# One addend instead of two in the norm of group B, and priority for its chain and for the out projection's additions

## The chip, the cores and the metric

The kernel runs on one core of one Trainium2 chip. The metric is the device time of one execution in microseconds (us); lower is better. In the text, TensorE (PE) multiplies matrices, VectorE (DVE) does elementwise work, ScalarE (ACT) does activations and casts, GpSimd (POOL) helps with elementwise work, and SyncE (SP) issues most DMA transfers. Each engine works through its own instructions in a fixed order and waits on semaphores for the others.

## The reference

One encoder layer on an input of 1 x 1024 tokens x 1024 channels, in float32. What matters here is the middle of it: two attention groups of 512 channels each, an RMS norm for each group, one out projection, and the residual sum.

```python
hn = rmsnorm(h, norm_mix[l])
proj = jnp.einsum('bsd,de->bse', hn, w_in[l])
...
o_a = window_gqa_sink(qa, ka, va, sink[l])
o_b = neighbourhood_attention(qb, kb, vb, rpb[l])
mix = jnp.concatenate([rmsnorm(o_a, norm_a[l]), rmsnorm(o_b, norm_b[l])], axis=-1)
h = h + jnp.einsum('bse,ed->bsd', mix, w_out[l])
hn = rmsnorm(h, norm_ffn[l])
h = h + conv_gated_mlp(hn, w_gate[l], w_up[l], conv_w[l], conv_b[l], w_down[l])
```

where `rmsnorm(x, g)` is `x * rsqrt(mean(x * x) + 1e-6) * g` over the channels.

## The kernel before, in words

Channels lie on the 128 partitions and the 1024 tokens along the free axis, in two halves of 512 (`tsl(h)`). Each float32 matmul is done as three fast ones: an operand is split into a high part (a cast on ScalarE) and a low part (a subtraction on VectorE), and a **block** is the three products high x high, high x low, low x high, each 128x512 (L113 to L115). A product of four blocks makes one half of one output tile out of 512 input channels, in one PSUM bank.

The order on TensorE is written by hand. The other four engines' orders are made by a planner at build time, which takes the instructions by priority (normally program order) as soon as its own model says that they are ready; a piece inside `tc.high_priority(offset=500)` is taken as if it stood 500 places earlier. Whatever order it makes is then fixed, and an engine waits at each instruction until that one may run.

**Attention with filler.** While the attention units of groups A and B run, a generator (`rest`, `fill(n)`) puts blocks of other matmul work between them. First these are the input projections, and at the end `OutA`, the half of the out projection that belongs to group A: for each of eight output tiles d it takes two products (halves h = 0, 1) of `mg[0:4]`, each into a bank of the tag `pj`, of which there are two. The addition at L490 reads the bank, adds the input tile `xr` (loaded by a DMA at L486), writes `h1[d]` and so frees the bank for the product after the next.

**Norm of group B.** `mix[4]` to `mix[7]` hold the four tiles of group B. Their squares are summed in `square_b` (L700 to L707) into `sums["b"]` for tiles 4 to 6; the squares of the last tile go into `last` (L744 to L746). `inverse_narrow` (L145) sums over the channels on TensorE: for each of four groups of 128 tokens it multiplies every addend with a column of ones, giving one column each (L150), then takes the square root on ScalarE (L153) and the reciprocal on VectorE (L154). `widen` (L157) spreads the result over 128 partitions by four more matmuls (L161). The norm itself is at L765 to L767: on VectorE a scaling of `mix[4 + i]` that reads the wide result, on ScalarE the cast to the high part `mg[4 + i]`, on VectorE the subtraction for the low part, for four tiles in each half.

The hand-written order around it, on TensorE, is: the last attention matmul, five blocks of `OutA` (`fill(5)`, L756), the sums of both halves (L757), four blocks (`fill(4)`), `widen` of half 0, three blocks (`fill(3)`), `widen` of half 1, and then all blocks of `OutA` that are left.

**Group B's out projection.** After that (loop of L857) come sixteen products of `mg[4:8]` with the other half of `w_out`, for half 0 and then for half 1, in six banks; L816 adds each to `h1[d]`, L819 and L821 square and sum for the next norm. The weights for d = 0 and 1 are loaded early (`load_wo`, L748), those from d = 2 on into memory that the attention stage gives back. In the same loop, and after it, the first weights of the gated MLP are made: `pure` loads and splits `w_gate`, and `head_weights` forms sums of `w_gate` and `w_up` blocks on VectorE (L843, L835). The MLP follows, and it is matmul after matmul to the end.

Of the kernel before, what the change touches and what calls it, by code (L numbers as in the profile page):

```python
# [15 lines left out]
AF = mybir.ActivationFunctionType  # L16
ALU = mybir.AluOpType
# [34 lines left out]
def hybrid_layer(tc, xT, w_in, w_out, w_gate, w_up, w_down, small, sink, rpb, consts, rope, out):  # L52
    nc = tc.nc
    with ExitStack() as ctx:
# [13 lines left out]
        def big(name, tag, dt=F32):  # L68
            return lpool.tile([128, S], dt, name=name, tag=tag, bufs=slots[tag])

        def tmp(name, dt=F32, n=S):
            return tpool.tile([128, n], dt, name=name, tag="t", padded_shape=[128, S + 2])

        def bank(name, tag):
            return psum.tile([128, HALF], F32, name=name, tag=tag)

        f32 = lambda ap: ap.bitcast(F32)
        tsl = lambda h: slice(h * HALF, (h + 1) * HALF)
# [38 lines left out]
        def product(ps, ws, xs, h):  # L117

            for i, (w, x) in enumerate(zip(ws, xs, strict=True)):
                block(ps, w, x, h, i == 0, i == len(ws) - 1)  # L120
                yield
# [23 lines left out]
        def inverse_narrow(sqs, dim, tag):  # L145

            ps = bank("ss", tag)
            for c in range(4):
                for i, sq in enumerate(sqs):
                    nc.tensor.matmul(ps[:, c:c + 1], sq[:, c * 128:(c + 1) * 128], ones[:, 0:1], start=c == 0 and i == 0,  # L150
                                     stop=i == len(sqs) - 1, skip_group_check=True)
            v = cpool.tile([128, 4], F32, name="v4", tag="v4", bufs=4)
            nc.scalar.activation(v, ps[:, 0:4], AF.Sqrt, bias=eps, scale=float(D) / dim)  # L153
            nc.vector.reciprocal(v, v)  # L154
            return v
# [86 lines left out]
        mix = [None] * 8  # L242
# [200 lines left out]
        mg, h1, norm = [None] * 8, [None] * KT, {}  # L443

        class Project:
# [6 lines left out]
            def run(self):  # L452
                self.t = tmp("t")
                if self.m < 17:
                    for h in range(2):
                        ps = bank("pj", "pj")
                        yield from product(ps, self.w, xg, h)
                        evacuate(self.t, ps, h, self.grid)
                else:

                    ps = [bank("pj", "pj") for _ in range(2)]
                    for k in range(KT):
                        for h in range(2):
                            block(ps[h], self.w[k], xg[k], h, k == 0, k == KT - 1)
                            yield
                        if k % 2:
                            mg[k // 2] = split(mix[k // 2], "mg", "xg")
                    for h in range(2):
                        evacuate(self.t, ps[h], h, self.grid)
# [5 lines left out]
        class OutA:  # L475
# [6 lines left out]
            def run(self):  # L482
                d = self.d
                h1[d] = big("h1", "mix" if d < 4 else "op")
                xt = tmp("xr")
                nc.sync.dma_start(xt, xT[d])  # L486
                for h in range(2):
                    ps = bank("pj", "pj")
                    yield from product(ps, self.w, mg[0:4], h)
                    nc.vector.tensor_tensor(h1[d][:, tsl(h)], ps, xt[:, tsl(h)], op=ALU.add)  # L490

            def post(self):
                pass
# [1 line left out]
        def fill(jobs):  # L495
            jobs[0].load()
            before = None
            for i, job in enumerate(jobs):
                if i + 1 < len(jobs):
                    jobs[i + 1].load()  # L500
                for n, _ in enumerate(job.run()):
                    yield
                    if n == LAG and before is not None:
                        before.post()
                        before = None
                before = job
            before.post()
# [190 lines left out]
        sums = {}  # L698
# [43 lines left out]


        last = tmp("sq")  # L744
        for h in range(2):
            nc.scalar.activation(last[:, tsl(h)], mix[7][:, tsl(h)], AF.Square)  # L746

        def load_wo(d, pools):  # L748
            raw = pools.tile([128, 4, 128], F32, name="raw", tag="raw", bufs=2 if pools is wpool else 3, padded_shape=[128, 4 if pools is wpool else 8, 128])
# [4 lines left out]
            return [(t[:, 0, j, :], t[:, 1, j, :]) for j in range(4)]  # L754

        fill(5)  # L756
        vb2 = [inverse_narrow([sums["b"][:, tsl(h)], last[:, tsl(h)]], 512, "pt") for h in range(2)]  # L757
        fill(4)
        mg[4:8] = [(big("mgh", "xg", F32R), big("mgl", "xg", F32R)) for _ in range(4)]
        for h in range(2):  # L760
# [96 lines left out]
        for h in range(2):  # L857
            for d in range(KT):
                if h == 0 and d + 2 < KT:
                    wo.append(load_wo(d + 2, fpool))  # L860
                ps = bank("pj", ("o", "s", "pj")[(h * KT + d) % 3])
# [365 lines left out]
        for i, (p, j, c) in enumerate(order):  # L1227
# [6 lines left out]
            ps = banks[p, j]  # L1234
# [118 lines left out]
```

## Time and profile before

| | |
|---|---|
| median of 3 runs | 1128.92 us (1128.06 to 1130.89) |
| the profiled execution, its own time | 1127.34 us |
| its span in the profile | 1125.6 us |
| TensorE busy | 96% of the span |
| VectorE busy | 76% |
| ScalarE busy | 49% |

Three views of the profile are used. The windows view gives, for a stretch of the span, how long each engine was busy in it, with the number of its instructions, the granted TensorE clock (1.00 is full), and the DMA load. The timeline lists instructions by start; where one sat behind idle time of its engine, brackets give that idle time and what ended it. The issues view lists DMA transfers with their size and their time to landing. All times in the views are microseconds from the start of the span.

### The profile page before, as it was taken

The page shows a single profiled execution, that of the slowest core. Times are in us where ns is not written, and L with a number is a line of the kernel's source. Part 1 is how long each engine was busy: PE and PEld are TensorE (multiplying, and loading weights), DVE is VectorE, ACT ScalarE, POOL GpSimd, SP SyncE. Part 2 cuts the span into 40 slices and gives each one's busy share as a digit, 9 for nine tenths or more (in the row PEclk, how much of TensorE's full clock was granted, in tenths as well). Part 3 has the DMA queues.
Part 4 walks back from the last instruction along what each step waited for, and adds up shares of the span by engine and source line. Part 5 has one row for each costly group of instructions (what it writes and reads, how often), then busy time and mean ns, then how long its engine had stood idle before and what let it go on. Part 6 is the DMA issues. An engine that isn't in the chain of part 4 may idle for free.

```text
span 1125.6 us, 14912 instructions
## 1 busy us (share of the span) xinstructions
PE 1086.2 (96%) x5124; PEld 903.0 (80%) x5124; DVE 852.4 (76%) x1549; ACT 548.3 (49%) x1033; POOL 105.7 (9%) x186
## 2 busy tenths in 40 slices
PE   8969999999999999999999999999999999999995
PEld 6858888888878877888788888888888878888884
DVE  6557888766689666989988778877877868797843
ACT  7235767655667433445434334334343645543531
POOL 0212332233223100000000000000000000000001
PEclk8989999999999999999999999999999999999997
DMA  7253220333215316412443223222322799875823
GB/s 266 65 122 80 53 57 29 84 92 87 75 31 148 103 47 211 163 47 78 166 160 122 105 92 123 102 103 94 122 103 94 244 302 294 268 221 174 272 83 144
DMA packets 67708, 147.03 MB, mean 131 GB/s; under 512 B 8112, under 2 KB 16816, under 8 KB 67632
## 3 DMA queue, kind: packets, MB, share of 16 engines
q1 hardware_dynamic: 57552, 121.04, 34.6%
q10 hardware_dynamic: 10080, 25.04, 5.9%
q8 instruction: 40, 0.66, 0.2%
q14 instruction: 36, 0.29, 0.1%
HBM read 103.58 MB, written 28.57 MB: 117 GB/s over the span
## 4 chain that ended last, share of the span: by engine, by line
PE 86%; DVE 7%; DMA 3%; ACT 2%; issue 2%; SPq 0%; POOLq 0%; ACTq 0%; DVEq 0%
PE pj L113 7%; PE pj L114 7%; PE pj L115 7%; PE dn L797 6%; PE dn L799 6%; PE dn L798 6%; PE z L799 5%; PE z L797 5%; PE z L798 5%; PE x L797 3%; PE x L799 3%; PE x L798 3%; PE s L273 3%; PE y L799 3%; PE y L797 3%; PE y L798 3%
## 5 line engine op out<-in xcount | busy, mean ns | idle before, releaser
L797 PE MATMUL dn<-xd,whi 128*128 128x512 f32 x308 | 120.2, 390 | 1.1 <-ACT c L1218 1.1
L786 ACT ACTIVATE whi<-ws 128x512 fp32r<-128x512 f32 (+1 forms) x100 | 60.1, 622 | 123.9 <-DVE ws L903 76.3
L799 PE MATMUL dn<-xd,wlo 128*128 128x512 f32 x308 | 119.8, 389 | 0.0
L798 PE MATMUL dn<-xd,whi 128*128 128x512 f32 x308 | 119.8, 389 | 0.0
L799 PE MATMUL z<-hg,wlo 128*128 128x512 f32 x264 | 103.1, 390 | 0.7 <-DVE wlo L787 0.7
L113 PE MATMUL pj<-xgh,whi 128*128 128x512 f32 x248 | 103.4, 417 | 0.0
L797 PE MATMUL z<-hg,whi 128*128 128x512 f32 x264 | 102.9, 390 | 0.0
L798 PE MATMUL z<-hg,whi 128*128 128x512 f32 x264 | 102.7, 389 | 0.0
L299 ACT ACTIVATE p<-p,nm 128x385 f32<-128x385 f32 (+3 forms) x128 | 75.1, 586 | 56.3 <-DVE nm L295 52.3
L115 PE MATMUL pj<-xgh,wlo 128*128 128x512 f32 x248 | 97.7, 394 | 0.0
L114 PE MATMUL pj<-xgl,whi 128*128 128x512 f32 x248 | 97.5, 393 | 0.0
L303 POOL TENSOR_SCALAR p<-p,sm 128x384 f32<-128x384 f32 (+1 forms) x128 | 73.5, 588 | 237.3 <-DVE sm L301 218.2
L787 DVE TENSOR_TENSOR wlo<-raw,whi 128x512 fp32r<-128x512 f32 (+1 forms) x102 | 66.3, 669 | 22.7 <-ACT whi L786 22.5
L787 DVE TENSOR_TENSOR wlo<-ws,whi 128x512 fp32r<-128x512 f32 (+1 forms) x100 | 66.7, 681 | 19.5 <-ACT whi L786 19.5
L309 DVE TENSOR_TENSOR pl<-pt,ph 128x384 fp32r<-128x384 f32 (+2 forms) x108 | 63.1, 588 | 23.2 <-ACT ph L308 22.1
L786 ACT ACTIVATE whi<-raw 128x512 fp32r<-128x512 f32 (+1 forms) x102 | 60.4, 611 | 41.4 <-DMA raw<-in_w_down_dram 18.4
L1108 ACT ACTIVATE xd<-xd 128x512 fp32r<-128x512 f32 x77 | 47.3, 627 | 58.0 <-DMA xd<-x 56.5
L308 ACT ACTIVATE ph<-pt 128x384 fp32r<-128x384 f32 (+2 forms) x108 | 55.3, 514 | 38.2 <-PE pt L408 30.8
L1209 POOL TENSOR_TENSOR y<-y,wide 128x512 f32<-128x512 f32 x4 | 5.1, 1283 | 727.0 <-ACT y L1208 727.0
L799 PE MATMUL y<-hg,wlo 128*128 128x512 f32 x176 | 68.7, 390 | 0.5 <-DVE wlo L787 0.5
L797 PE MATMUL x<-hg,whi 128*128 128x512 f32 x176 | 68.7, 390 | 0.0
L799 PE MATMUL x<-hg,wlo 128*128 128x512 f32 x176 | 68.5, 389 | 0.0
(199 smaller groups left out, 2657.8 us busy)
## 6 DMA issues: line engine op xcount, KB each, us to landing
xd<-x SPq DMA_DIRECT2D x77, 256.0 KB, 5.1
raw<-in_w_down_dram SPq DMA_DIRECT2D x72, 256.0 KB, 3.4
raw<-in_w_gate_dram SPq DMA_DIRECT2D x22, 512.0 KB, 3.5
raw<-in_w_up_dram SPq DMA_DIRECT2D x22, 512.0 KB, 4.0
x<-c ACTq DMA_DIRECT2D x22, 512.0 KB
raw<-in_w_in_dram SPq DMA_DIRECT2D x32, 256.0 KB, 3.2
raw<-in_w_down_dram SPq DMA_DIRECT2D x36, 192.0 KB, 3.8
x<-t ACTq DMA_DIRECT2D x11, 512.0 KB, 2.6
```

The source lines that it names most:

```text
L113: nc.tensor.matmul(ps, w[0], x[0][:, tsl(h)], start=first, stop=False)
L114: nc.tensor.matmul(ps, w[0], x[1][:, tsl(h)], start=False, stop=False)
L115: nc.tensor.matmul(ps, w[1], x[0][:, tsl(h)], start=False, stop=last)
L299: nc.scalar.activation(p[:, j, 0:e], p[:, j, 0:e], AF.Exp, bias=nm, scale=-1.0, accum_out=sm[:, j:j + 1])
L303: nc.gpsimd.tensor_scalar(p[:, i, 0:m], p[:, i, 0:m], sm[:, i:i + 1], 1.0, op0=ALU.mult, op1=ALU.mult)
L308: nc.scalar.activation(ph[:, 0:n], ps[:, 0:n], AF.Copy)
L309: nc.vector.tensor_tensor(pl[:, 0:n], ps[:, 0:n], f32(ph[:, 0:n]), op=ALU.subtract)
L786: nc.scalar.activation(hi, src, AF.Copy)
L787: nc.vector.tensor_tensor(lo, src, f32(hi[:, :, :]), op=ALU.subtract)
L797: nc.tensor.matmul(ps, w[0], x[0], start=first and i == 0, stop=False, skip_group_check=True)
L798: nc.tensor.matmul(ps, w[0], x[1], start=False, stop=False, skip_group_check=True)
L799: nc.tensor.matmul(ps, w[1], x[0], start=False, stop=last and i == len(ws) - 1, skip_group_check=True)
```

## The change

Three edits. The squares of the last tile are added to `sums["b"]` on VectorE, half by half, so that `inverse_narrow` has one addend for each half instead of two. The squares, these additions, and the chain of sums, square roots and reciprocals stand in `tc.high_priority(offset=500)`. So does each of `OutA`'s additions.

```diff
@@ OutA.run
                     ps = bank("pj", "pj")
                     yield from product(ps, self.w, mg[0:4], h)
-                    nc.vector.tensor_tensor(h1[d][:, tsl(h)], ps, xt[:, tsl(h)], op=ALU.add)
+                    with tc.high_priority(offset=500):
+                        nc.vector.tensor_tensor(h1[d][:, tsl(h)], ps, xt[:, tsl(h)], op=ALU.add)
@@ norm of group B
         last = tmp("sq")
-        for h in range(2):
-            nc.scalar.activation(last[:, tsl(h)], mix[7][:, tsl(h)], AF.Square)
+        with tc.high_priority(offset=500):
+            for h in range(2):
+                nc.scalar.activation(last[:, tsl(h)], mix[7][:, tsl(h)], AF.Square)
+                nc.vector.tensor_tensor(last[:, tsl(h)], last[:, tsl(h)], sums["b"][:, tsl(h)], op=ALU.add)
...
         fill(5)
-        vb2 = [inverse_narrow([sums["b"][:, tsl(h)], last[:, tsl(h)]], 512, "pt") for h in range(2)]
+        with tc.high_priority(offset=500):
+            vb2 = [inverse_narrow([last[:, tsl(h)]], 512, "pt") for h in range(2)]
         fill(4)
```

## The prediction

> **What bounds the kernel now.** I read the page's engine totals first, then the chain that ended last by engine, then the waits, and last the windows and the timeline of the stretch that the change touches.
>
> ```profile
> PE 1086.2 (96%) x5124; PEld 903.0 (80%) x5124; DVE 852.4 (76%) x1549; ACT 548.3 (49%) x1033; POOL 105.7 (9%) x186
> PE 86%; DVE 7%; DMA 3%; ACT 2%; issue 2%; SPq 0%; POOLq 0%; ACTq 0%; DVEq 0%
> ```
>
> TensorE is the bound: busy for 96% of the span, and 86% of the chain. Time can come only from where TensorE works slowly or waits. The next table is the windows view of TensorE alone, cut at the starts of its groups: sums of group B's norm (L150), four `OutA` blocks, first widening, three blocks, second widening, two blocks of output tile 6, half 1 (with a wait), four blocks of tile 7, half 0, a hole, four blocks of tile 7, half 1, and the first product with `mg[4:8]`.
>
> ```profile
> 403.35:407.00 3.65, 3.65 (x33) 0.95 0.20 75
> 407.00:411.26 4.26, 4.26 (x13) 0.64 0.34 123
> 411.26:412.07 0.81, 0.81 (x9) 1.00 0.00 0
> 412.07:414.23 2.16, 2.16 (x12) 1.00 0.00 0
> 414.23:415.04 0.81, 0.81 (x9) 1.00 0.00 0
> 415.04:416.94 1.90, 1.64 (x10) 1.00 0.00 0
> 416.94:420.00 3.06, 3.05 (x12) 1.00 0.00 0
> 420.00:423.18 3.18, 0.00 (x1) 1.00 0.00 0
> 423.18:427.63 4.45, 4.45 (x12) 0.62 0.00 0
> 427.63:430.35 2.72, 2.72 (x13) 1.00 0.51 165
> ```
>
> The columns are the length of the stretch, TensorE's busy time with its instructions, the granted clock, and the DMA load. Twelve matmuls take 2.72 us at full clock (0.68 a block), but 4.26 and 4.45 us at granted clocks of 0.64 and 0.62. Both slow stretches follow one without full-width matmuls: 3.65 us of one-column sums, and a hole of 3.18 us. The hole, as the timeline tells, ends with an addition:
>
> ```profile
> 423.18 0.50 PE L113 MATMUL pj<-mgh,whi 128*128 128x512 f32 x1 [3.18 <-DVE h L490]
> ```
>
> ```profile
> 401.51 0.69 DVE L490 TENSOR_TENSOR h<-pj,xr 128x512 f32<-128x512 f32 x1
> ...
> 408.67 0.69 DVE L490 TENSOR_TENSOR h<-pj,xr 128x512 f32<-128x512 f32 x1 [4.20 <-PE pj L115]
> ...
> 412.36 2.06 DVE L765 SCALAR_TENSOR_TENSOR mixb<-mixb,par,sw 128x512 f32<-128x512 f32 x3 [2.85 <-PE sw L161]
> ...
> 416.20 0.68 DVE L490 TENSOR_TENSOR h<-pj,xr 128x512 f32<-128x512 f32 x1
> ...
> 422.44 0.68 DVE L490 TENSOR_TENSOR h<-pj,xr 128x512 f32<-128x512 f32 x1
> ...
> 430.55 0.69 DVE L816 TENSOR_TENSOR h<-pj,h 128x512 f32<-128x512 f32 x1 [2.03 <-PE pj L115]
> ```
>
> The additions at 416.20 and 422.44 belong to tile 6. They stand behind the norm on VectorE, and each frees the bank for a product of tile 7: TensorE starts at 416.94 and 423.18, right after them. VectorE idles 4.20 and 2.85 us just before the norm, and then has too much at once.
>
> **Edit 1: one addend.** Sixteen of 32 sums leave TensorE. A row for exactly 16 of them is the norm of group A:
>
> ```profile
> 297.17 1.84 PE L150 MATMUL ss<-ones,sq 128*128 128x1 f32 x16
> 298.87 0.48 PE L113 MATMUL pj<-xgh,whi 128*128 128x512 f32 x1
> ```
>
> They take 298.87 - 297.17 = 1.70 us, so the sums shrink from 3.65 to 1.70: **1.95 us** saved. The matmul behind them has its ordinary 0.48 us, without a slow stretch; so I let the slow stretch of 4.26 us become three blocks in 2.16 us plus one of 0.68, which is 2.84: **1.42 us** saved. Two additions of 0.69 come to VectorE.
>
> ```profile
> 401.47 1.16 ACT L746 ACTIVATE sq<-mixb 128x512 f32<-128x512 f32 x2 [0.76 <-DVE mixb L436]
> 430.50 0.63 ACT L752 ACTIVATE wo<-raw 128x512 fp32r<-128x512 f32 x1 [7.92 <-DMA raw<-in_w_out_dram]
> ```
>
> The squares end near 402.1 and 402.6. In the changed order the two additions stand right behind the L490 of 401.51, so they end near 402.9 and 403.5. TensorE wants the first sum at 403.35 and the second half's at 404.2: both are there. They are covered by VectorE's idle 4.20 us; without that cover they would cost 1.4 us.
>
> The Trainium skill, page "TensorE: Matmul & The Clock Gate", section "Part 1: The HAM clock gate (the "warmup" mystery)", says that the clock falls to half after an idle window of about 3.4 us and comes back after a busy window as long. By it two slow stretches would cost an estimated 3.4 us together, where the rows above give (4.26 - 2.84) + (4.45 - 2.72) = 3.15, and the sum below would be 9.3 instead of 9.0. The trace agrees only in part: a hole of 3.18 us sufficed, and 3.65 us of narrow matmuls counted as idle although the profile has TensorE busy there. I go by the rows.
>
> **Edit 2: priority of the additions.** In the changed VectorE order both additions of tile 6 stand among the first half's norm: one behind the first scaling, one behind the fourth. Tile 7's stand behind the first half's last low part and before the second half's last pieces. TensorE's new times are: sums to 405.05, blocks to 407.89, widening (0.81) to 408.70, blocks (2.16) to 410.86, widening to 411.67. The first addition of tile 6 needs the block behind the first widening, so it can run near 409.7; the product that waits for its bank is due two blocks behind 411.67, near 413.2. The second has three scalings, two low parts and one addition ahead of it since 409.7, 6 x 0.69 = 4.1 us, and ends by 414.5; its bank is wanted at 415.9. Neither product waits. Then the ten blocks from 415.04 on take 10 x 0.68 + 0.12 (three blocks behind a widening took 2.16 instead of 2.04), 6.92 us, instead of 427.63 - 415.04 = 12.59: **5.67 us** saved. That is the hole, the wait at 416.94 and the second slow stretch together.
>
> What is queued behind these additions: they wait for TensorE, and the rest of the norm waits with them. The first half's last low part stands ahead of tile 7's additions, so the first product with `mg[4:8]` does not meet that wait. The second half's last pieces, some 2.5 us (three low parts and a scaling at 0.69), fall behind 418.6. They are wanted eight products later (8 x 2.72 = 21.8 us). They take the idle 2.03 us that VectorE had before the L816 of 430.55.
>
> **Edit 3: priority of the norm's chain.** Square roots and reciprocals keep their places; behind the addition of tile 5 the reciprocals end near 407.7, before the widening at 407.89. I cost it at nothing; one late reciprocal costs its lateness.
>
> **Queues.** SP's and POOL's orders stay. SP's load of tile 7's `xr` may wait for the addition of tile 5 near 407.3. The slowest landing of such a load is
>
> ```profile
> xr<-in_xT_dram SPq DMA_DIRECT2D x2, 512.0 KB, 7.8
> ```
>
> which would put it at 415.1, before tile 7's first addition at 416.2. The loads of `w_out` for tile 2 follow TensorE's last `OutA` block, and move with it:
>
> ```profile
> 427.82 4.39 SPq L750 DMA_DIRECT2D raw<-in_w_out_dram  x4
> ```
>
> They were cast at 430.50, 2.9 us behind 427.63; now near 421.5 to 422, behind the eighth cast of the norm, and wanted at 418.6 + 2 x 2.72 = 424.0.
>
> **Does the lead stay?** VectorE by stage (columns: length, PE, PEld, DVE, ACT, POOL, clock, DMA):
>
> ```profile
> 401.50:427.60 26.10, 22.66 (x108) 18.66 (x107) 14.79 (x25) 9.03 (x15) 0.00 (x0) 0.87 0.13 43
> 427.60:486.00 58.40, 58.40 (x275) 48.82 (x274) 46.59 (x76) 28.02 (x49) 0.00 (x0) 1.00 0.60 201
> 486.00:538.60 52.60, 52.34 (x230) 42.71 (x228) 52.12 (x83) 25.89 (x41) 0.00 (x0) 1.00 0.17 57
> ```
>
> From 486 to 538.6 VectorE is busy for 52.12 of 52.60 us: whatever it is late at 486 comes back one for one. Before 486 it has 11.3 + 11.8 us idle, and the change wants 9.0 + 1.4 of it. In the order before 486 one thing moves: the sums of weights for the MLP (L835) stand earlier, and three of their loads now share one buffer in turn. Their rows before:
>
> ```profile
> 475.19 0.33 SPq L792 DMA_DIRECT2D raw<-in_w_gate_dram  x1
> 477.95 0.69 DVE L835 TENSOR_TENSOR ws<-ws,raw 128x512 f32<-128x512 f32 x1 [0.79 <-DMA raw<-in_w_gate_dram]
> 479.16 0.68 DVE L821 TENSOR_TENSOR s<-s,s 128x512 f32<-128x512 f32 x1
> 481.19 0.95 PE L150 MATMUL ss<-ones,s 128*128 128x1 f32 x8
> 483.04 0.17 DVE L154 RECIPROCAL v<-v 128x4 f32<-128x4 f32 x1
> 484.87 1.05 PE L161 MATMUL sw<-cst,v 128*128 128x128 f32 x8
> ```
>
> A load lands in 477.95 - 475.19 = 2.76 us. On the clock of before (the lead left out), the second can be issued near 476.3, some 1.1 us behind the 475.19 of before, for the sum of 0.69 moved ahead and a short wait of it. It lands at 479.1; its sum of weights and the last sum of squares take 2 x 0.69 and end near 480.5, for 481.19. The third is issued near 479.8 and lands near 482.6; its sum and the reciprocal end near 483.5, for 484.87. The slack of 0.7 and 1.4 us covers it. I take 0.3 us for such edges, between 0 and the 3 us of the second rival.
>
> **Sum:** 1.95 + 1.42 + 5.67 = 9.04, less 0.3: 8.7 us. Against the profiled execution's 1127.34 this is 1118.6; it lies 1.58 below the median of 1128.92, which becomes **1120.2 us**.
>
> **The rivals.**
> 1. *The clock still falls.* Sums and widenings stand within 8.3 us (403.35 to 411.67), and the gate may count low work instead of idleness. For it: the 3.65 us of busy sums counted. Against it: the row of 298.87. One slow stretch stays: 1120.2 + 1.4 = 1121.6. By the page's rule it could not come, since no idle window of 3.4 us is left.
> 2. *Part comes back where VectorE is full.* The serial loads land in 5 us instead of 2.76: the last sum ends at 482.7, 1.5 late, and the reciprocal is late by as much again, 3 us in all: 1123.2. For it: 52.12 of 52.60. Against it: the slack.
> 3. *The additions don't free the banks.* Tile 7's `xr` lands late or tile 6's additions are held by the norm's own waits; then only edit 1 pays, 3.4 us: 1125.5. Against it: 1 us of slack at the slowest landing.
> 4. *Slower.* The same chain of three serial loads, at 9 us each: the second lands at 485.3, the last sum ends at 486.7, 5.5 late; the third is issued at 486.0, lands at 495.0, and the reciprocal ends at 495.9 for 490.4, 5.5 more; 11.0 - 9.0 = 2.0: 1130.9. The loss is twice (L - 3.5) for a load of L, so it decides from about 8.0 us. For it: 7.8 us was seen once, for twice the size; against it: 2.76 at this place.
>
> **How the numbers follow.** A measurement of this kernel can tell about 0.3%, 3.4 us. Forecast 0.66, rival 1 0.08, rival 2 0.13 (0.02 of it within 0.3%), rival 3 0.06 (half within), rival 4 0.07. Faster: 0.66 + 0.08 + 0.11 + 0.03 = 0.88; same 0.05; slower 0.07. The range goes from 1117.6 (no edge cost, and 2.3 us of run-to-run spread) to 1125.2, past rival 2; what it leaves out is rival 4, half of rival 3 and some at the low end.
>
> **What would show it.** Sixteen L150 matmuls in 1.7 us behind the attention; a granted clock of 1.00 in the blocks behind them; no wait of TensorE for L490; the first product with `mg[4:8]` near 418.6; the first L816 near 421.6; the sums of the next norm near 472.2 and its widening near 475.9. If those two come with waits, rival 2 or 4 holds.

## The result, and the profile after

The changed kernel takes 1122.09 us (median of 6 runs, 1120.15 to 1124.73), the kernel before 1128.59 us beside it (6 runs, 1128.06 to 1131.67). The ratio is 0.9936, with a 95% interval of 0.9920 to 0.9952: between 5.4 and 9.0 us faster. The forecast of 1120.2 us was 1.9 us too low, and the measured time lies within its range. The profiled execution took 1121.43 us, 5.9 us less than the 1127.34 us of before; forecast were 8.7.

TensorE's row of the engine totals, and the chain that ended last, by engine:

```profile
PE 1081.4 (97%) x5108; PEld 898.9 (80%) x5108; DVE 853.4 (76%) x1551; ACT 548.2 (49%) x1033; POOL 106.0 (9%) x186
PE 84%; DVE 7%; DMA 5%; ACT 2%; issue 2%; SPq 0%; POOLq 0%; ACTq 0%; DVEq 0%
```

Sixteen matmuls are gone (5124 to 5108), and TensorE is still the bound. The share of DMA in the chain has grown from 3% to 5%; that comes back below. The windows view of TensorE for the changed kernel, cut at the start of the sums, their end, the end of the second widening's first block, the first product with `mg[4:8]`, and 12 matmuls later; the row behind the dots is a place far behind, in the down projection (length, busy time with instructions, granted clock, DMA share and rate):

```profile
403.32:405.02 1.70, 1.70 (x17) 1.00 0.08 24
405.02:411.77 6.75, 6.75 (x40) 1.00 0.22 78
411.77:418.53 6.76, 6.76 (x32) 1.00 0.00 0
418.53:421.25 2.72, 2.72 (x14) 1.00 0.53 169
...
921.13:923.85 2.72, 2.72 (x6) 0.50 0.81 273
```

The sums take 1.70 us instead of 3.65, and from them to the first product with `mg[4:8]` there is no idle time and no fallen clock. That product starts at 418.53; 418.6 was forecast, and before it was 427.63. VectorE's timeline shows how:

```profile
402.11 1.29 DVE L749 TENSOR_TENSOR sq<-sq,sqb 128x512 f32<-128x512 f32 x2
...
406.00 0.69 DVE L491 TENSOR_TENSOR h<-pj,xr 128x512 f32<-128x512 f32 x1 [1.39 <-PE pj L115]
...
409.62 0.69 DVE L491 TENSOR_TENSOR h<-pj,xr 128x512 f32<-128x512 f32 x1
...
413.40 0.68 DVE L491 TENSOR_TENSOR h<-pj,xr 128x512 f32<-128x512 f32 x1
...
416.01 0.69 DVE L491 TENSOR_TENSOR h<-pj,xr 128x512 f32<-128x512 f32 x1
...
418.73 0.69 DVE L491 TENSOR_TENSOR h<-pj,xr 128x512 f32<-128x512 f32 x1
...
421.45 0.69 DVE L820 TENSOR_TENSOR h<-pj,h 128x512 f32<-128x512 f32 x1 [0.17 <-PE pj L115]
```

(Lines behind L490 have moved by one to four: the addition is now L491, L816 is L820, L835 is L839, L1218 is L1222.) The two new additions end at 403.4, hidden. Tile 6's additions stand at 409.62 and 413.40, among the norm's pieces, before the products that need their banks; tile 7's stand at 416.01 and 418.73. The first addition behind the new products is at 421.45 (421.6 was forecast).

So the stretch that the change touches went as forecast, to a tenth or two of a microsecond. The sums of the next norm start at 472.56 and its widening at 476.27, 0.4 us behind the forecast of 472.2 and 475.9. What is missing beyond that was lost later. The lead of TensorE over the kernel before, as the difference of the starts of the same matmul in the two traces, is 427.63 - 418.53 = 9.10 at the first product with `mg[4:8]` and 8.6 at the next norm's sums (481.19 and 472.56). Then comes the down projection, some 500 us later. Changed kernel:

```profile
918.43 0.39 PE L803 MATMUL dn<-xd,wlo 128*128 128x512 f32 x1
919.97 0.63 ACT L1112 ACTIVATE xd<-xd 128x512 fp32r<-128x512 f32 x1 [1.59 <-DMA xd<-x]
920.50 0.58 ACT L1222 ACTIVATE c<-dn 128x512 f32<-128x512 f32 x1
921.13 0.79 PE L801 MATMUL dn<-xd,whi 128*128 128x512 f32 x1 [2.32 <-ACT c L1222]
928.41 0.39 PE L802 MATMUL dn<-xd,whi 128*128 128x512 f32 x1
```

Kernel before:

```profile
926.51 0.39 PE L799 MATMUL dn<-xd,wlo 128*128 128x512 f32 x1
926.86 0.63 ACT L1108 ACTIVATE xd<-xd 128x512 fp32r<-128x512 f32 x1 [1.14 <-DMA xd<-x]
927.40 0.58 ACT L1218 ACTIVATE c<-dn 128x512 f32<-128x512 f32 x1
928.03 0.50 PE L797 MATMUL dn<-xd,whi 128*128 128x512 f32 x1 [1.13 <-ACT c L1218]
933.84 0.39 PE L798 MATMUL dn<-xd,whi 128*128 128x512 f32 x1
```

TensorE waits there for a bank that ScalarE's copy (`c<-dn`) must empty. The copy is queued behind a cast of `xd`, and the cast waits for a DMA. The wait is 2.32 us instead of 1.13, and behind it the granted clock is 0.50 (last row of the windows above). The lead falls from 8.08 (926.51 - 918.43) to 6.90 (928.03 - 921.13) and then to 5.43 (933.84 - 928.41): 2.65 us are lost at this one place. Between the traces' ends 6.0 remain (spans of 1125.6 and 1119.6).

### The profile page after: what moved, and what is told of

Same layout as the page of the kernel before. It is cut to its first block, busy times and chain, and to the rows that moved or that the text cites. A ratio compares the mean times of both kernels' runs of the same rounds, so it can differ in the third digit from the quotient of the medians.

```text
span 1119.6 us, 14885 instructions
## 1 busy us (share of the span) xinstructions
PE 1081.4 (97%) x5108; PEld 898.9 (80%) x5108; DVE 853.4 (76%) x1551; ACT 548.2 (49%) x1033; POOL 106.0 (9%) x186
## 4 chain that ended last, share of the span: by engine, by line
PE 84%; DVE 7%; DMA 5%; ACT 2%; issue 2%; SPq 0%; POOLq 0%; ACTq 0%; DVEq 0%
PE pj L113 7%; PE pj L114 7%; PE pj L115 7%; PE dn L801 5%; PE dn L803 5%; PE dn L802 5%; PE z L803 5%; PE z L801 4%; PE z L802 4%; PE x L801 3%; PE s L273 3%; PE x L803 3%; PE x L802 3%; PE y L803 3%; PE y L801 3%; PE y L802 3%
## 5 line engine op out<-in xcount | busy, mean ns | idle before, releaser
L791 DVE TENSOR_TENSOR wlo<-raw,whi 128x512 fp32r<-128x512 f32 (+1 forms) x102 | 66.2, 670 | 22.9 <-ACT whi L790 22.7
L791 DVE TENSOR_TENSOR wlo<-ws,whi 128x512 fp32r<-128x512 f32 (+1 forms) x100 | 66.7, 681 | 18.6 <-ACT whi L790 18.5
L801 PEld LDWEIGHTS dn<-xd,whi 128*128 128x128 f32 x308 | 58.2, 189 | 14.8 <-ACT c L1222 2.7
```

The costliest lines, as they stand in the source:

```text
L791: nc.vector.tensor_tensor(lo, src, f32(hi[:, :, :]), op=ALU.subtract)
L801: nc.tensor.matmul(ps, w[0], x[0], start=first and i == 0, stop=False, skip_group_check=True)
```

## The experiments

Three questions were open. Is each part of the change worth what the prediction gave it? Is the lead lost again at the down projection by a fixed mechanism (rival theory), or was that one draw of a wait that varies anyway? And is a fallen clock behind a gap a certain cost, or one that some executions escape?

Two lengths serve to compare the traces, because they hold no difference that a trace brings with it from its beginning. The **hand-over** runs from the first sum (L150) to the first product with `mg[4:8]`: 427.63 - 403.35 = 24.28 us before, 418.53 - 403.32 = 15.21 changed. The **next stretch** runs from there to the second sums of the next norm: 481.19 - 427.63 = 53.56 before, 472.56 - 418.53 = 54.03 changed. The windows view has each in one row. Each ratio below is against the kernel before, timed beside the variant on the same chip; the medians of different experiments are less sure to compare, since chips and executions differ.

### Each part alone

Edit 1 alone, the kernel before with

```diff
             nc.scalar.activation(last[:, tsl(h)], mix[7][:, tsl(h)], AF.Square)
+            nc.vector.tensor_tensor(last[:, tsl(h)], last[:, tsl(h)], sums["b"][:, tsl(h)], op=ALU.add)
...
-        vb2 = [inverse_narrow([sums["b"][:, tsl(h)], last[:, tsl(h)]], 512, "pt") for h in range(2)]
+        vb2 = [inverse_narrow([last[:, tsl(h)]], 512, "pt") for h in range(2)]
```

> Edit 1 alone: the last squares are added on VectorE and each half has one addend; no priorities. My theory: the sums take 1.7 us instead of 3.65 and the blocks behind them keep the full clock, so the first product with mg[4:8] starts 3.3 us earlier than the 427.63 of before, near 424.3, while the wait of some 3.2 us for the additions of tile 6 and the slow stretch behind it stay; time 1128.6 - 3.3 = 1125.3, up to 1 us more if the start of the down projection takes some of it back as it did in the changed kernel. Rival (the wait only grows, since VectorE's norm is what ends last there): wait 5 us or more, first product near 427, time 1127.5 to 1128.6.

Measured: 1125.79 us, ratio 0.9968 (0.9947 to 0.9989), 3.6 us by the ratio. The hand-over in the windows view, and the wait at its end in the timeline:

```profile
404.27:423.55 19.28, 15.81 (x84) 1.00 0.10 31
```

```profile
420.70 0.50 PE L113 MATMUL pj<-mgh,whi 128*128 128x512 f32 x1 [3.21 <-DVE h L490]
```

The hole is there as it was before, 3.21 us long, but the clock stays at 1.00 behind it. The hand-over is 19.28 us. Against the changed kernel's 15.21 the waits for the banks cost 4.07 us: 0.26 and 3.21 us of idleness, and the 0.6 us that are left over, in which the matmuls take up their pace again.

Edit 2 alone, the kernel before with

```diff
-                    nc.vector.tensor_tensor(h1[d][:, tsl(h)], ps, xt[:, tsl(h)], op=ALU.add)
+                    with tc.high_priority(offset=500):
+                        nc.vector.tensor_tensor(h1[d][:, tsl(h)], ps, xt[:, tsl(h)], op=ALU.add)
```

> Priority for OutA's additions alone; two addends as before. My theory: the wait for L490 goes, and with it the slow stretch behind it, 5.7 us; the sums still take 3.65 us and the blocks behind them stay slow; first product with mg[4:8] near 422.0; time 1128.6 - 5.7 = 1122.9, up to 2.7 us more if the start of the down projection takes some back. Rival (the additions need the earlier sums to pay, because VectorE has too little time): a wait of 1 us or more for L490 stays, first product after 423, time above 1125.

Measured: 1125.75 us, ratio 0.9965 (0.9945 to 0.9984), 4.0 us by the ratio. Its hand-over:

```profile
403.03:420.08 17.05, 17.05 (x101) 1.00 0.13 47
```

No wait is left in it, and the clock did not fall behind the 32 sums this time. So 17.05 - 15.21 = 1.84 us is what the sixteen extra sums cost by themselves. Of the hand-over's gain, 24.28 - 17.05 = 7.2 us in the profiled traces, the times show only about half. Part of that 7.2 is the two slow stretches of the trace of before, which not every execution of that kernel has (below). In this trace TensorE loses 1.0 us in the next stretch, and at the down projection it waits 1.84 us with a slow clock behind it:

```profile
922.31 0.50 PE L798 MATMUL dn<-xd,whi 128*128 128x512 f32 x1 [1.84 <-ACT c L1219]
```

The priority on the norm's chain (edit 3) does nothing: with one addend and priority on the additions alone, the planner makes the same program, instruction for instruction.

### The sums with everything else changed

The changed kernel with each half's addend summed twice, so that TensorE has 32 sums again. The sum is doubled and divided by twice the number, which gives the same norm:

```diff
-            vb2 = [inverse_narrow([last[:, tsl(h)]], 512, "pt") for h in range(2)]
+            vb2 = [inverse_narrow([last[:, tsl(h)], last[:, tsl(h)]], 1024, "pt") for h in range(2)]
```

> The changed kernel with each half's one addend summed twice and the scale halved: 32 sums on TensorE as before, everything else as in the changed kernel. If the clock falls because of the length of the one-column stretch: granted clock near 0.64 in the four blocks behind it, 3.4 us slower than the changed kernel up to the first product with mg[4:8] (near 421.9 instead of 418.53). If the sums only cost their own time: clock 1.00 there, first product near 420.5, 1.95 us.

Measured: 1124.46 us, ratio 0.9953 (0.9933 to 0.9973). Its hand-over:

```profile
401.63:420.24 18.61, 18.61 (x100) 0.91 0.09 32
```

Same work as in edit 2 alone, and 18.61 instead of 17.05 us, at a mean clock of 0.91: one slow stretch, which costs 1.56. Nothing differs in what TensorE does there; in the one trace the clock fell behind the 32 sums, in the other it did not. The table of all traces, below, shows why. At the down projection TensorE waited for no copy in this trace.

### The bank instead of the order

If the hole comes from the bank alone, other banks remove it without any priority. The kernel before, with the sums of tile 7 in banks of another tag:

```diff
-                    ps = bank("pj", "pj")
+                    ps = bank("pj", "s" if d == KT - 1 else "pj")
```

> The kernel before, with one thing changed: output tile 7's two sums are put into banks of another tag, so their products no longer wait for the bank that the additions of output tile 6 free; additions and norm keep their order on VectorE, and there are still 32 sums. If the wait for the bank is the whole of the hole, it goes without any priority: the wait of 0.26 us at 416.94 and the hole of 3.18 us at 423.18 are gone (3.4 us), the first product with mg[4:8] starts near 424.2, or near 422.4 where no slow stretch follows; time 1125.5 (1122 to 1128), and the late additions show up later, if at all, as a wait of the first product that needs their h. If the additions are wanted for another reason (their h, or the norm's pieces behind them), TensorE waits there just the same and the time is that of the kernel before. The clock behind the 32 sums may fall again (it did in four of five traces with 32 sums).

Measured: 1125.2 us, ratio 0.9977 (0.9956 to 0.9998). Hand-over (windows), then the timeline:

```profile
402.86:421.50 18.64, 18.64 (x100) 0.91 0.14 48
```

```profile
428.49 0.50 PE L115 MATMUL pj<-mgh,wo 128*128 128x512 f32 x1 [0.92 <-DVE wo L753]
...
925.08 0.50 PE L797 MATMUL dn<-xd,whi 128*128 128x512 f32 x1 [3.20 <-ACT c L1218]
```

The hole is gone without priority: 18.64 us, the same as the changed order with 32 sums, again with one slow stretch behind the sums. So the bank was what TensorE waited for, not the results. Part is paid back: the new products overtake the making of their weights and wait 0.92 us for a low part, and in this trace the down projection has the longest wait of all, 3.20 us, with a slow clock behind it.

### The same programs again

The kernel before, timed and profiled once more, and one further trace of it:

> The kernel before unaltered, for a second trace of it. By chance of the clock: at least one of the two slow stretches (behind the sums near 407, behind the hole near 423) is missing or shorter in this trace, and the lead of the changed kernel against it is less than 9 us. By rule of the clock: both are there, 1.4 and 1.7 us.

> The kernel before once more, for one more draw of the clock. If a fall of the clock behind these gaps is chance: a slow stretch behind the 3.65 us of one-column sums likely (four of five traces), behind the hole of some 3.2 us as often as not (two of four traces). If both follow by rule, both are there, 1.4 and 1.7 us.

Measured for the first: 1131.61 us, ratio 1.0021 (1.0002 to 1.004) against the other runs of the same program on that chip. So a ratio here may be off by 0.2% beyond what its interval says. The execution of the third trace took 1128.06 us. The first's windows and timeline:

```profile
403.73:426.42 22.69, 19.22 (x100) 0.92 0.11 39
```

```profile
929.27 0.50 PE L797 MATMUL dn<-xd,whi 128*128 128x512 f32 x1 [2.57 <-ACT c L1218]
```

In the third trace the hand-over is 426.72 - 404.02 = 22.70 us, and the wait at the copy 2.23 us.

In both the hand-over of the unchanged program is 1.58 us shorter than in the trace from which the prediction was made: the clock fell behind the sums, but not behind the hole of 3.2 us. And in both TensorE waits 2.57 and 2.23 us for the copy at the down projection, without any lead to lose; behind the first the clock fell as well. So a wait of this length needs no lead, and nothing here shows that the lead brought about the 2.32 us in the changed kernel.

The changed kernel again, timed and profiled, and one further trace:

> The changed kernel unaltered, for a second trace beside the others on one chip. My theory after the first runs: whether the granted clock falls behind a gap of some 3.2 to 3.7 us is chance (one_addend kept the full clock behind a wait of 3.2 us, additions_first behind 3.6 us of one-column sums), so the change is worth 7.6 us in removed work and waits for sure and up to 3.15 us more when the clock would have fallen. Here: no slow stretch between 403 and 430, lead at the first product with mg[4:8] 9 us over the first trace of before (less what the start of the program shifts), and a wait for the copy of the down projection's first product of 0 to 2.5 us near 919. Time 1120 to 1123. Rival (the clock falls by rule behind such gaps): the lead is the same, and all later differences come from the down projection alone.

> The changed kernel once more, for one more draw of two things. The hand-over: the first product with mg[4:8] 8.5 to 9.1 us earlier than in the kernel before, with no slow stretch behind the 16 sums (as in the three traces of 16 sums with the changed order so far). The down projection's first copy: TensorE's wait for ScalarE's copy anywhere from 0 to 2.6 us, and a slow stretch behind it only if it is over about 1.8 us. If instead the lead always comes back there by a fixed mechanism, the wait is 2.3 us and the slow stretch of about 1.7 us follows again.

The 7.6 us "for sure" in the first expectation is a slip: the prediction's 9.04 less its two clock terms is 5.9. Measured: 1120.12 us, ratio 0.9933 (0.9911 to 0.9955); the execution of the third trace took 1121.38 us. Windows of the first, hand-over and next stretch (the second row with all engines: PE, PEld, DVE, ACT, POOL), then its timeline:

```profile
403.72:418.93 15.21, 15.21 (x85) 1.00 0.12 40
...
418.93:474.26 55.33, 54.85 (x246) 44.13 (x244) 46.05 (x76) 26.91 (x48) 0.00 (x0) 1.00 0.57 195
```

```profile
437.60 0.63 ACT L755 ACTIVATE wo<-raw 128x512 fp32r<-128x512 f32 x1 [1.33 <-DMA raw<-in_w_out_dram]
...
452.07 0.69 DVE L839 TENSOR_TENSOR ws<-ws,raw 128x512 f32<-128x512 f32 x1 [2.34 <-DMA raw<-in_w_gate_dram]
...
468.30 0.50 PE L801 MATMUL x<-hg,whi 128*128 128x512 f32 x1 [0.33 <-DVE h L820]
...
921.16 0.50 PE L801 MATMUL dn<-xd,whi 128*128 128x512 f32 x1 [1.33 <-ACT c L1222]
```

The third trace has a hand-over of 15.20 us and a wait of 1.52 us at the copy.

The hand-over is the same to 0.01 us. The waits at the copy are 1.33 and 1.52 us, without a slow clock behind them. But a second cost shows: the next stretch is 55.33 us in the first and 54.39 in the third trace, instead of 53.56. Set side by side with a trace of the kernel before, matmul by matmul, the first of these loses its 1.77 us at two places. Some 0.7 us go at 438 to 439, where TensorE waits for a weight of `w_out` that ScalarE casts late, because its load had not landed (the row of 437.60). The rest goes from 468 on: VectorE has stood 2.34 us at a sum of weights (`ws`) whose load has not landed, and the norm's work behind it, and the additions that free TensorE's banks (the wait at 468.30), are late.

### The copy on another engine

If the copy's place behind a DMA-fed cast on ScalarE makes TensorE wait, the copy on VectorE does not. In the changed kernel (twice) and in the kernel before:

```diff
-                nc.scalar.activation(c_at(j), ps, AF.Copy)
+                nc.vector.tensor_copy(c_at(j), ps)
```

> The changed kernel with the copies of the down projection's first four products (L1222 of it) on VectorE instead of ScalarE, where they stand behind a cast that waits for a DMA. My theory: in the changed kernel TensorE's lead of 8.1 us shrinks by 2.7 us at 918 to 924, since that copy is queued behind the cast of a transfer (wait 2.32 us) and the clock falls behind the wait (1.4 us). With the copies elsewhere the wait and the slow stretch go: 2.7 to 3.7 us faster than the changed kernel, near 1118.7. Rival (the transfers themselves limit that stretch): TensorE waits a little later for the operands xd or the weights, total wait again 1.5 to 2.5 us, and the time stays within 1 us of 1122.1.

> The changed kernel with the copies of the down projection's first four products on VectorE, again, now beside the changed kernel on one chip. If the copy behind a DMA-fed cast takes back part of the lead: 1 to 3 us faster than changed_again. If its first result (1120.0) was the chip: within 1 us of changed_again.

> The kernel before with the same copies on VectorE. If the copy costs the same whatever the lead is: as much faster than before as evict_again is than changed_again, 1 to 3 us. If the larger wait comes only with the lead (the transfers are later against TensorE): 1.1 us at most, the wait of the first trace of before, and the change is worth more with the copies moved than without.

Measured: on the changed kernel 1120.01 us, ratio 0.9915 (0.9895 to 0.9936), and 1118.67 us, ratio 0.9918 (0.9891 to 0.9945); on the kernel before 1128.17 us, ratio 1.0002 (0.9985 to 1.0019). The waits at the copy were 1.34 and 0.34 us in the changed kernel, and 1.32 us (for the cast of `xd` itself) in the kernel before, all without a slow clock behind them. From the two timelines of the changed kernel with the copy on VectorE, the first and then the second:

```profile
452.81 0.69 DVE L839 TENSOR_TENSOR ws<-ws,raw 128x512 f32<-128x512 f32 x1 [2.74 <-DMA raw<-in_w_gate_dram]
...
469.04 0.50 PE L801 MATMUL x<-hg,whi 128*128 128x512 f32 x1 [1.08 <-DVE h L820]
```

```profile
450.47 0.69 DVE L839 TENSOR_TENSOR ws<-ws,raw 128x512 f32<-128x512 f32 x1 [1.86 <-DMA raw<-in_w_gate_dram]
```

On the changed kernel the medians differ by about 1.5 us for the copy's place (1120.12 to 1118.67 on the same chip), but the intervals overlap, so this gain is not shown; on the kernel before there is nothing that can be measured. With the first trace the second cost is seen well: a wait of 2.74 us for the load, and a next stretch of 55.49 us, nearly all of the excess lost from 469 on; with 1.86 us it is 53.78.

### The sum of weights on another engine

The kernel just shown, with the four sums of weights that read `w_gate`'s first half taken off VectorE:

```diff
                 g = load_raw(w_gate[f, :, 0:4], 4)
-                sub(t, t, g)
+                nc.gpsimd.tensor_tensor(t, t, g, op=ALU.subtract)
```

> The changed kernel with the first down product's copies on VectorE (as evict_on_vector) and, new, the four sums ws<-ws,raw (w_up's sums less a loaded half of w_gate) on GpSimd in place of VectorE, so that no norm's work stands on VectorE behind the landing of these loads. In the changed order the first of these sums waited 1.7 to 2.7 us at 450 to 453, and from the first product with mg[4:8] to the second sums of the next norm the changed kernel took 54.03, 55.33, 54.39, 55.49 and 53.78 us in five traces against 53.56 to 53.58 in all with the order of before. If that wait on VectorE is the cause, the stretch is 53.6 again, TensorE waits for no addition there, and the time is about 1 us below the two runs with the copies on VectorE (1120.01 and 1118.67): near 1118.3 (1116.5 to 1120), ratio near 0.991. If VectorE's bulk of work is the cause (the norm's last pieces and the low parts that fall behind the hand-over), the stretch stays between 53.8 and 55.5, less at most 0.7 for the sum taken off VectorE. If GpSimd is too slow for them, the low part behind the sum waits for GpSimd and TensorE for that part, and the time goes up.

Measured: 1118.30 us, ratio 0.9904 (0.9884 to 0.9924), 10.8 us by the ratio; the profiled span is 1115.9 us. The windows (second row with all engines) and the timeline:

```profile
403.64:418.85 15.21, 15.21 (x85) 1.00 0.12 40
...
418.85:472.41 53.56, 53.56 (x246) 44.59 (x245) 46.37 (x74) 27.17 (x48) 9.08 (x4) 1.00 0.63 211
```

```profile
454.05 2.49 DVE L809 TENSOR_TENSOR hg<-h,hg 128x512 fp32r<-128x512 f32 x4
455.15 2.54 POOL L850 TENSOR_TENSOR ws<-ws,raw 128x512 f32<-128x512 f32 x1 [2.90 <-DMA raw<-in_w_gate_dram]
...
468.87 1.29 POOL L850 TENSOR_TENSOR ws<-ws,raw 128x512 f32<-128x512 f32 x1 [3.73 <-DMA raw<-in_w_gate_dram]
468.92 1.78 DVE L825 TENSOR_TENSOR s<-s,s 128x512 f32<-128x512 f32 x1
```

The next stretch is 53.56 us again, as with the order of before, and TensorE does not wait in it; GpSimd now does the waiting. VectorE is busy for 46.37 us in it, as in the trace that took 55.33 (46.05). That speaks for the wait in its queue, and against the bulk of its work, as what made the stretch longer. It is not shown: this is one trace, and among the others one reached 53.58 with a wait of 1.71 us (the changed kernel with 32 sums). Its median is the lowest of all, but does not lie clearly apart from the 1118.67 without this last edit.

### All traces side by side

Hand-over and next stretch are differences of starts, as defined above; the wait is the idle time in front of the down projection's matmul that waits for the first copy (in "before, copy on VectorE" for the cast of `xd`); "slow" says that the next matmuls ran at half pace.

| kernel | sums | hand-over | slow stretches in it | next stretch | wait at the copy |
|---|---|---|---|---|---|
| before | 32 | 24.28 | 2: sums, hole | 53.56 | 1.13 |
| before, again | 32 | 22.69 | 1: sums | 53.57 | 2.57, slow |
| before, third trace | 32 | 22.70 | 1: sums | 53.57 | 2.23 |
| before, copy on VectorE | 32 | 24.28 | 2: sums, hole | 53.58 | 1.32 |
| one addend | 16 | 19.28 | 0 (hole there) | 53.56 | 2.40 |
| other bank | 32 | 18.64 | 1: sums | 54.79 | 3.20, slow |
| additions first | 32 | 17.05 | 0 | 54.53 | 1.84, slow |
| changed, 32 sums | 32 | 18.61 | 1: sums | 53.58 | none |
| changed | 16 | 15.21 | 0 | 54.03 | 2.32, slow |
| changed, again | 16 | 15.21 | 0 | 55.33 | 1.33 |
| changed, third trace | 16 | 15.20 | 0 | 54.39 | 1.52 |
| changed, copy on VectorE | 16 | 15.20 | 0 | 55.49 | 1.34 |
| the same, again | 16 | 15.21 | 0 | 53.78 | 0.34 |
| the same, sums on GpSimd | 16 | 15.21 | 0 | 53.56 | none |

The hand-over takes only a few values, and they add up: 15.21; 1.8 more with 32 sums (17.05); 1.6 more for each slow stretch (18.6); 4.07 more with the waits for the banks (18.6 + 4.07 = 22.7), and with the second slow stretch 24.28.

When the clock falls can be read from the traces too. In each trace the changes of the granted clock lie whole multiples of 3.41 us apart, and each slow stretch of the table lasts 3.41 us. So each trace has a grid of windows of 3.41 us, and the grid lies at another place against the program in every trace. These are rows of the windows view cut at the grid, for TensorE's products of 512 columns alone (the second number is the time that it was busy with them). They show, for the kernel before, the sums, the window behind them, the hole, and the window behind it; then the hole of "before, again", the sums of "additions first", the sums of the changed kernel, and the wait at the down projection in "additions first":

```profile
403.25:406.66 3.41, 0.26 (x2) 1.00 0.24 91
406.66:410.07 3.41, 3.07 (x7) 0.50 0.43 153
420.32:423.73 3.41, 0.55 (x2) 1.00 0.00 0
423.73:427.14 3.41, 3.41 (x9) 0.50 0.00 0
...
418.58:421.99 3.41, 1.77 (x8) 1.00 0.00 0
422.00:425.41 3.41, 1.84 (x8) 1.00 0.00 0
...
401.58:404.99 3.41, 1.61 (x8) 1.00 0.49 163
404.99:408.40 3.41, 1.88 (x8) 1.00 0.17 47
...
402.07:405.48 3.41, 1.87 (x9) 1.00 0.34 130
...
920.40:923.81 3.41, 1.56 (x8) 1.00 0.82 269
```

The clock falls at the end of a window in which these products took little time. Around the hand-over and the first copies of the down projection, twelve windows of the fourteen traces were followed by a slow one; they hold 0.24 to 1.56 us of products. All others hold 1.55 us or more. So a fall needs some 3.41 - 1.56 = 1.85 us of one window without such products. Sums of 1.70 us cannot take so much (in the seven traces with 16 sums, every window that holds sums has 1.87 us or more of products), while 3.49 us of sums nearly always do, and a hole of 3.2 us escapes when the grid cuts it near its middle. What differs between executions is where the grid lies.

## Why the prediction was right, and where it was wrong

**Edit 1's sums: right.** 1.95 us forecast, 1.8 us measured (17.05 - 15.21), and the two additions are hidden.

**Edit 2's waits: right.** Both waits went, by the order that the prediction read from VectorE's queue; tile 6's additions start at 409.62 and 413.40, where a start near 409.7 and an end by 414.5 were forecast. The 5.67 us were 3.94 of waits and resumption and 1.73 of slow clock; the first part measures 4.07. Rival 3 (the additions don't free the banks) is out. That the bank was the thing waited for is shown by the run with another bank.

**Edit 3: right**, it does nothing.

**The clock terms: charged as certain, and somewhat too large.** The prediction let both slow stretches go and took 1.42 + 1.73 = 3.15 us for them, as if the kernel before paid them each time. The size of one is right (1.6 us), but whether it is paid depends on where the grid lies, and the trace from which the prediction was made was one with both. Behind 32 sums the clock fell in 6 of 7 traces, behind the hole of 3.2 us in 2 of 5; by these few traces the kernel before pays (6/7 + 2/5) x 1.58 = 2.0 us on average. The timed executions are more. Each has a mean granted clock; twice its missing share, times the span, is the time at half clock, 34.7 us on average in 86 executions of the kernel before and 28.8 in 15 of the changed one. The 5.9 us between them are 1.7 stretches, give or take 0.3, and 1.7 x 1.58 = 2.7 us is an estimate for the whole kernel, which has the down projection in it as well. The average gain of the hand-over is then an estimated 1.8 + 4.07 + 2.7 = 8.6 us (7.9 by the few traces) instead of 9.04. The kernel pays none of it after the change: no slow stretch in the 6 traces of the changed order with 16 sums, so that rival 1 (the clock still falls) did not occur. Its ground was partly right, since the one-column sums do count as low work, but 1.70 us of them are too short.

**The edges: mis-sized.** For VectorE's later work 0.3 us were taken off. In the five traces of the changed order with 16 sums and the sums of weights on VectorE the next stretch is 0.2 to 1.9 us longer than before, 1.0 us on average. Part of it is the mechanism of rival 2 in a small form (a sum of weights in front of the norm's work waits for its load), but not at the place named there; part, 0.7 us in one trace, is a late load of `w_out`. The rival's chain of loads stood at 475 to 485 on the clock of before; the long wait was at the first of these sums, now at 450, which the prediction did not price. With this the estimate is 8.6 - 1.0 = 7.6 us (6.9 by the few traces), and the ratio gives 7.2, the medians 6.5. Rival 4 (slower) needed loads of 8 us; nothing like it was seen.

**What the prediction left out.** "Does the lead stay?" looked up to 538.6 and at VectorE alone. At 920, on ScalarE, stands a wait that the profiled execution of before met at its lowest among the three traces of that program (1.13 us, against 2.23 and 2.57) and that of the changed kernel at its highest among three (2.32, against 1.33 and 1.52). That explains the 2.65 us between the two profiles, but nothing shows that it is a cost of the change: over three traces each, the wait is 2.0 us before and 1.7 changed. The forecast of 1120.2 was nearly right because all that was missed is small, and not because errors cancelled: the clock terms were too large by some 0.4 us (1.1 by the few traces) and the edges too small by 0.7, and both make the forecast too low. The rest is within what repeated runs of one program differ.

What stays open: why the DMA of `xd` lands early or late, what sets the place of the clock's grid in an execution, and how much of the longer next stretch each late load costs. No run settles these.

## What to carry to other kernels

Price a slow clock behind a gap as a chance, not as a term, unless the gap is so long or so short that the place of the grid does not matter: look at it in several traces of the same program, or give it its share and widen the range. Compare traces by the length of a stretch between two landmarks of the program, not by the time since the start of the trace; here fourteen traces whose spans scatter by several microseconds fell on six values. And where a priority moves work forward on an in-order engine, look at each load-fed instruction that moves with it: it may now wait in front of something that TensorE needs.

## What the runs showed of the hardware that was not expected

**The clock falls at the ends of windows of 3.41 us, and a wait of 1.84 us can be enough.** By the table alone it looks like chance: behind waits of 1.84, 2.32, 2.57 and 3.20 us at the down projection the clock fell, behind 2.23 and 2.40 us it did not, and never behind 1.52 us or less. By the grid, each fall follows a window with at most 1.56 us of products of 512 columns, and no window with more was followed by one. One-column matmuls, in which TensorE is busy by the profile, do not save a window: behind 3.49 to 3.65 us of them the clock fell in 6 of 7 traces, behind 1.70 us in none of 7. One slow stretch costs 1.6 us. All this was seen at these two places of one program; elsewhere in it, with matmuls of other widths, the limit was not worked out. The Trainium skill, page "TensorE: Matmul & The Clock Gate", section "Part 1: The HAM clock gate (the "warmup" mystery)", has a free-running window of about 3.4 us and says that the clock halves after at least one idle window. The grid of 3.41 us agrees with the free-running window; that a whole window must be idle does not fit the fall behind the wait of 1.84 us, in whose window TensorE was busy for 1.56 us.

**GpSimd and VectorE hold each other up.** The same 128x512 subtraction took GpSimd 1.29 us at 468.87, and 2.54 us at 455.15, where VectorE was in the middle of four subtractions that read two tiles of SBUF each: these end near 456.5, and 456.5 + 1.3 gives 457.8, near its end at 457.7 (spans of GpSimd are rough in this profile). In turn the addition of VectorE at 468.92, which began just behind GpSimd's, took 1.78 us instead of 0.69. The Trainium skill, page "SBUF — State Buffer", section "Who interferes with whom", says that a VectorE instruction with two SBUF inputs contends with a GpSimd instruction that reads SBUF, and calls the shared port an exclusive lock; the two rows agree with it.
